# Router sums on two halves of the array's columns, and squares added by VectorE instead of GpSimd casts and TensorE sums

## The chip, the cores and the metric

One core of a Trainium2 chip runs the whole program: two transformer blocks on 512 tokens of width 1024, all in float32. The metric is the device time of one execution in microseconds (us). A difference is read against the median of the runs of the kernel before.

## The reference, cut to what matters

```python
# first block
mix = concat([attn, conv]) @ w_out
x = x + gt1 * mix                                   # x1, 8 row blocks of 128 columns, kept transposed
h2 = rms_norm(x, g_norm2) * (1 + sc2) + sh2
x = x + gt2 * hier_moe(h2, ...)                     # router: h2 @ [w_rg | w_re], 4 + 32 logits a token
x = rms_norm(x, g_final)
# second block
proj = rms_norm(h, norm_mix_pre) @ w_in             # among it the value projection sb_v
...
mix = (gate_sb * (sb @ w_sb_out) + gate_gla * (o @ w_gla_out)) @ w_o
h = h + rms_norm(mix, norm_mix_post)                # the mean of squares of mix, over 8 row blocks
ffn = (gelu(dwconv(rms_norm(h) @ w_up)) * (rms_norm(h) @ w_gate)) @ w_down
```

An RMS norm needs the sum of squares over all 1024 columns of a token. Activations lie transposed (columns on the 128 partitions), so such a sum runs across partitions and is made by TensorE: a product of a matrix of ones with the squares.

## The kernel before, in words

Weights stream from HBM through raw buffers. A class `Stream` splits each weight tile into a rounded part and a remainder (`split`, L223 on ScalarE and L224 by whichever engine `ws.lo` names), and a product in split form is three matmuls (`mm3`, L310 to L312). The order of instructions on each engine is set by a scheduler when the program is built; nobody writes it out. Within an engine, instructions run in that order.

Three places matter here.

**The router (L790 to L923).** For each of 8 row blocks m, the output projection of block m + 1 runs on TensorE (`pw` or `p`, L310 to L312) while VectorE and ScalarE turn block m into `x` (L793), `xs` (scaled, L796) and `sq` (squared, L798 or L800). Then `router` adds two float32 products: the logits, 36 columns of stationary weights, into bank `plg` (L808), and the sum of squares, 32 columns of ones, into another bank, `plq`, from partition 64 (L809). Four transposes `pth` (L817) follow. After the last block, ScalarE and VectorE copy the two sums into `lgT` (L919, L920), and `plgt` (L923) turns them over for the routing.

**The experts' end (L1419 to L1529).** After the experts, a loop over overflow blocks is branched over. Then the last expert's rows are added into x: pairs of products `psx` (L1306, L1307), VectorE's `x` (L1299), ScalarE's `sq` and `uh` and VectorE's `ul` (L1480). Sums of squares `pss` (L1276) and the second block's value projection (`pva`, `pvb`) run between them on TensorE. There `ws.lo` is GpSimd's `tensor_tensor`: GpSimd makes the remainder of four weight tiles, `wsplit`. GpSimd also makes `ut` (L1479). At the end VectorE works out the norm's factor (L1287 to L1292), builds a diagonal `dg` (L1526), and TensorE spreads it with `pspread` (L1529), twice.

**The mix before the feed-forward part (L2170 to L2200).** For each of 8 row blocks m and two column halves a (260 and 256 tokens), 24 matmuls make `pmix`; ScalarE reads it out twice, as `mx` (L2181) and as the square (L2182). A class `Sums` collects squares, and `flush` (L1641) adds each by a float32 product with ones, `psum` (L1643), after the next half's products. ScalarE (L1648) turns the sum into the norm's factor. Meanwhile the weights of block m + 2 are split into one of two `wsplit` tiles.

```python
    def mix_out(m, a):
        ps = pso.pop((m, a))
        act(part(mx[m], a), ps, AF.Copy, scale=cc("norm_mix_post", m))
        act(part(sqo[m], a), ps, AF.Square)
        su.add(a, sqo[m])
```

Of the kernel before, what the change touches and what calls it, by code (L numbers as in the profile page):

```python
# [11 lines left out]
F32 = mybir.dt.float32  # L12
# [3 lines left out]
OP = mybir.AluOpType  # L16
# [4 lines left out]
P = 128  # L21
T = 512
D = 1024
KD = D // P
NM = 16
L = T + NM
# [5 lines left out]


COLS = [
    ("b_mod", 48), ("g_norm1", 8), ("conv_b", 4), ("conv_ln_g", 4), ("conv_ln_b", 4),
    ("conv_w", 4 * 31), ("g_norm2", 8), ("w_router", 8 * 36), ("c", 8),
    ("g_final", 8), ("norm_mix_pre", 8), ("b_gk", 4), ("gla_head_norm", 2),
    ("norm_mix_post", 8), ("norm_ffn_pre", 8), ("conv_w2", 22 * 3), ("conv_b2", 22),
]
# [154 lines left out]
def build(nc, tc, I, out, dbg=None):  # L194
    with ExitStack() as ctx:
        _build(ctx, nc, tc, I, out, dbg or {})


def _build(ctx, nc, tc, I, out, dbg):
    mm = nc.tensor.matmul  # L200
    transpose = nc.tensor.transpose
    act = nc.scalar.activation
    tt = nc.vector.tensor_tensor
# [105 lines left out]
    def mm3(ps, lh, ll, rh, rl, first, last):  # L309
        mm(ps, lh, rh, start=first, stop=False)  # L310
        mm(ps, lh, rl, start=False, stop=False)  # L311
        mm(ps, ll, rh, start=False, stop=last)  # L312
# [10 lines left out]
    def cc(name, i=0, n=1):  # L323
        o = COFF[name][0] + i
        return cpk1[:, o:o + n] if o < NCOL1 else cpk2[:, o - NCOL1:o - NCOL1 + n]
# [5 lines left out]
    ones = const.tile([P, P], F32, name="ones")  # L331
# [44 lines left out]
    def p1(name="p1"):  # L376
        return pp.tile([P, 512], F32, name=name, tag="p1", bufs=4)
# [105 lines left out]
    ws = Stream(plan, castp, 3, nmoe)  # L483
# [62 lines left out]
    for k in range(KD):  # L546
        sq = big.tile([P, T], F32, name="sq", tag=("sq", "t512")[k % 2], bufs=2)
# [211 lines left out]
    wr = lambda k: cc("w_router", 36 * k, 36)  # L759
# [24 lines left out]
    plg = []  # L784
# [18 lines left out]
    def router(st):  # L803
        m, sq, xs = st
        if m == 0:
            plg.extend((p1("plg"), p1("plq")))
            act(rs_[:, 0, 0:1], sq[:, 0:1], AF.Sqrt)
        mm(plg[0][0:36, :], wr(m), xs, start=(m == 0), stop=(m == KD - 1), skip_group_check=True)  # L808
        mm(plg[1][64:96, :], ones[:, 0:32], sq, start=(m == 0), stop=(m == KD - 1), skip_group_check=True)  # L809
        if m < KD - 1:  # L810
            token_major(m, xs)

    def token_major(m, xs):
        pt = p1("pth")
        for i in range(4):
            s = slice(i * P, (i + 1) * P)
            transpose(pt[:, s], xs[:, s], ident)  # L817
        for a in range(2):
            (copy if m % 2 and m < KD - 1 else lambda o, x: act(o, x, AF.Copy))(
                h2t[a][:, :2 * D].rearrange("p (i d) -> p i d", d=D)[:, :, m * P:(m + 1) * P],  # L820
                pt[:, a * 256:(a + 1) * 256].rearrange("p (i n) -> p i n", n=P))
# [77 lines left out]
    for m in range(KD):  # L899
        if m < 6:  # L900
            ps = pw[m]
            proj1(ws, mh, ml, ps, k=4, k0=4, first=False)
        else:
            ps = p1()
            proj1(ws, mh, ml, ps)
        if m in (2, 5):
            with tc.high_priority(offset=-1000), tc.issue_after(tap[0].ins):
                for _ in range(2):
                    next(mod)
        if behind:  # L910
            router(behind)
        behind = ev_x1(m, ps)
    next(mod)
    router(behind)
    for m in range(KD):
        dump(f"x1_{m}", xT[m])
# [4 lines left out]
    plg = p1("plgt")[:, :256].rearrange("p (i n) -> p i n", n=64)  # L921
# [320 lines left out]
    def weighted(psd, w, spare=False):  # L1242
        yh, yl = [(ep.tile([P, D], F32R, name="yx", tag="x", bufs=3) if spare else
                   yp.tile([P, D], F32R, name=n, tag=n)) for n in ("yh", "yl")]
        for n in range(2):
            s = slice(n * 512, (n + 1) * 512)
            act(yh[:, s], psd[n], AF.Copy, scale=w)  # L1247
            stt(yl[:, s], psd[n], w, yh[:, s].bitcast(F32), OP.mult, OP.subtract)  # L1248
        return yh, yl
# [64 lines left out]
    side, xs = [], {}  # L1314
# [99 lines left out]
    last = weighted(psd, wsl[:, q:q + 1])  # L1414
# [4 lines left out]
    with tc.For_i(0, n_over, 1) as o:  # L1419
# [5 lines left out]
        ws = Stream([(I["w_moe"][bass.ds(e, 1), i, :, :].rearrange("a p n -> (a p) n"), (2048,), False)  # L1425
                     for i in range(6)])
# [13 lines left out]
    ws = main  # L1440
# [14 lines left out]
                self.t = raw1.tile([P, 2048], dt, name="wsplit", tag="raw", bufs=2)  # L1455
            return self.t[:, :1024] if tag == "whi" else self.t[:, 1024:]

    ws.pool, ws.rc, ws.rings, ws.lo = Halves(), 2, ws.rings[:1], nc.gpsimd.tensor_tensor
    ws.rings[0][3], ws.pin = len(plan), nmoe + 1
    ws.hold_at(nmoe + 2)  # L1460
    ws.load()
# [103 lines left out]
    HP = ctx.enter_context(tc.tile_pool(name="H", bufs=1))  # L1565
# [7 lines left out]
    def t5(name, p=P):  # L1573
        return HP.tile([p, L], F32, name=name, tag="t5", bufs=4)
# [52 lines left out]
    def part(ap, a):  # L1627
        return ap[:, E[a][0]:E[a][1]]

    class Sums:  # L1630
# [7 lines left out]
        def add(self, a, sq):  # L1638
            self.pend[a].append(sq)

        def flush(self, a):  # L1641
            for sq in self.pend[a]:
                mm(self.ps[a], ones, part(sq, a), start=(self.n[a] == 0), stop=(self.n[a] == KD - 1))  # L1643
                self.n[a] += 1
            self.pend[a] = []

# [72 lines left out]
    for k0 in (0, 4):  # L1719
        for x in (nh, nl):  # L1720
            for a in range(2):
                for k in range(4):
                    mm(pl[a][32 * k:32 * k + 32], w[:, k0 + k, :], x[k0 + k][:, a * HF:(a + 1) * HF].bitcast(F32),
                       start=(k0 == 0 and x is nh), stop=(k0 > 0 and x is nl), skip_group_check=True)
# [290 lines left out]
    last = gv0_end(gv[:, 0])  # L2015
# [3 lines left out]
    last = gv1_end(gv[:, 1])  # L2019
# [90 lines left out]
    for d in range(2):  # L2110
        sqs = []
# [5 lines left out]
        for a in range(2):  # L2117
            for h in range(4):
                mm(pn[32 * h:32 * h + 32, a, :H5], ones[:, 0:32], ends(sqs[h])[:, a], start=(d == 0), stop=(d == 1),
                   skip_group_check=True)  # L2120
# [45 lines left out]
    su = Sums([t[:, 0], t[:, 1]])  # L2166
    r = HP.tile([P, L], F32, name="rstd2", tag="rstd2", bufs=2)
    wo, pso, sqo = {}, {}, {}

    def mix_mm(m, a):  # L2170
        if m not in wo:
            wo[m] = ws.nxt(P)
            sqo[m] = t5("sq")
        wh, wl = wo[m]
        ps = pso[m, a] = p1("pmix")[:, :E[a][1] - E[a][0]]
        for kk in range(KD):
            mm3(ps, wh[:, kk, :], wl[:, kk, :], part(mh[kk], a), part(ml[kk], a), kk == 0, kk == KD - 1)

    def mix_out(m, a):
        ps = pso.pop((m, a))  # L2180
        act(part(mx[m], a), ps, AF.Copy, scale=cc("norm_mix_post", m))  # L2181
        act(part(sqo[m], a), ps, AF.Square)  # L2182
        su.add(a, sqo[m])

    for m in range(KD - 2):
        for a in range(2):
            mix_mm(m, a)
            su.flush(a)
        for a in range(2):
            mix_out(m, a)  # L2190

    for a in range(2):
        for m in (KD - 2, KD - 1):
            mix_mm(m, a)
            su.flush(a)
            mix_out(m, a)
        su.flush(a)
        with tc.high_priority(offset=100):
            su.rstd(a, r, D)
# [8 lines left out]
    def h_gen(a):  # L2208
        for k in range(KD):
            with tc.high_priority(offset=200):  # L2210
                t, h, g = cp.tile([P, T], F32, name="t", tag="y", bufs=3)[:, :E[a][1] - E[a][0]], part(hT[k], a), cc("norm_ffn_pre", k)
                tt(t, part(mx[k], a), part(r, a), OP.mult)
                (nc.gpsimd.tensor_tensor if k in HPL else tt)(h, h, t, OP.add)
                act(part(nh[k], a), h, AF.Copy, scale=g)
                stt(part(nl[k], a), h, g, part(nh[k], a).bitcast(F32), OP.mult, OP.subtract)
            sq = t5("sq")
            act(part(sq, a), h, AF.Square)
            su.flush(a)
            su.add(a, sq)
            if k == KD - 1:  # L2220
                su.flush(a)
            yield
# [20 lines left out]
    def ffn_mm(m):  # L2243
        ps, pg = p2("pup"), p1("pg")
        if m == 0:
            wg, ws.order = None, True
            for a in range(2):
                g = h_gen(a)
                for _ in range(1):
                    next(g)  # L2250
                if a == 0:
                    wu = ws.nxt(P)
                for n, _ in enumerate(up_gen(wu, ps, (a,))):
                    if n == 4 and wg is None:
                        wg = ws.nxt(P)
                    next(g, None)
                wg = wg or ws.nxt(P)
                run(gate_gen(wg, pg, slice(256 * a, 256 * a + 256)))
            ws.order = False
        else:  # L2260
            run(up_gen(ws.nxt(P), ps))
            run(gate_gen(ws.nxt(P), pg))
        return ps, pg
# [89 lines left out]
    su = Sums([p1("psum"), p1("psum")])  # L2353
# [29 lines left out]
```

## Time and profile before

| what | value |
|---|---|
| median of 3 runs | 1812.47 us (1812.36 to 1816.58) |
| profiled execution, its own time | 1818.69 us |
| span of the profiled execution | 1816.9 us, 26870 instructions |
| TensorE busy in the span | 1745.1 us (96%) |
| VectorE, ScalarE, GpSimd busy | 881.3, 629.3, 109.6 us |
| mean granted TensorE clock | 0.978 |

The span runs from the first instruction's start to the last one's end; the execution's own time has 1.8 us more around it. TensorE's busy time overstates it, since the ends of its pipelined matmuls are modelled: where matmuls follow each other, the distance of their starts is what one costs. A row of the timeline gives start, duration, engine, line, operation, output and inputs, the shape, how many instructions it merges, and in brackets how long the engine had been idle and what ended that.

### The profile page before, as it was taken

How to read it: one execution, taken by the hardware profiler on the slowest of the kernel's cores; microseconds unless marked ns; L12 is line 12 of the kernel's file. 1: busy time of each engine (PE TensorE's matmuls, PEld its weight loads, DVE VectorE, ACT ScalarE, POOL GpSimd, SP SyncE). 2: the span in 40 equal slices, each digit the busy share in tenths (PEclk: the TensorE clock that was granted, in tenths of full speed). 3: DMA queues.
4: the chain of work that ended last, by engine and by line, in shares of the span. 5: the costliest groups of instructions: out<-in, count | busy, mean ns of one | idle time of the engine just before them, and what ended most of it. 6: DMA issues, size and time to landing. Idle time of an engine off the chain costs nothing.

```text
span 1816.9 us, 26870 instructions
## 1 busy us (share of the span) xinstructions
PE 1745.1 (96%) x10826; PEld 1263.2 (70%) x10826; DVE 881.3 (49%) x1597; ACT 629.3 (35%) x1141; POOL 109.6 (6%) x147
## 2 busy tenths in 40 slices
PE   7999997999999999998899999999999999999997
PEld 4776565444445444445788668989999899789985
DVE  6789654433333334235577742253332645335534
ACT  5226653211111111104567743242233633223322
POOL 2000010000000000003200100030000111001101
PEclk9989898999999999999999999999999999999998
DMA  8563253999999999930411012113222222222221
GB/s 327 199 242 136 89 216 130 380 409 409 408 411 360 385 408 410 412 128 27 159 67 49 24 47 93 47 63 128 102 100 87 70 91 78 100 93 93 94 87 64
DMA packets 73986, 328.01 MB, mean 181 GB/s; under 512 B 8019, under 2 KB 8403, under 8 KB 59652
## 3 DMA queue, kind: packets, MB, share of 16 engines
q1 hardware_dynamic: 72608, 320.36, 46.6%
q0 software_dynamic: 1248, 5.91, 0.9%
q8 instruction: 86, 1.41, 0.3%
q14 instruction: 40, 0.33, 0.0%
q10 hardware_dynamic: 4, 0.00, 0.0%
HBM read 321.98 MB, written 4.26 MB: 180 GB/s over the span
## 4 chain that ended last, share of the span: by engine, by line
PE 48%; DVE 3%; ACT 2%; DMA 1%; POOL 1%; issue 1%; DVEq 0%; ACTq 0%; POOLq 0%
PE p L1620 11%; PE pup L2232 7%; PE pq L1598 4%; PE pg L312 2%; PE pg L310 2%; PE pg L311 2%; PE pd L311 2%; PE pd L312 2%; PE pd L310 2%; PE pv L310 1%; PE pv L311 1%; PE pv L312 1%; PE pmix L310 1%; PE psum L1643 1%; PE pmix L312 1%; PE pmix L311 1%
## 5 line engine op out<-in xcount | busy, mean ns | idle before, releaser
L224 DVE TENSOR_TENSOR wsplit<-raw,wsplit 128x1024 fp32r<-128x1024 f32 (+1 forms) x140 | 167.4, 1198 | 250.6 <-ACT wsplit L223 244.7
L223 ACT ACTIVATE wsplit<-raw 128x1024 fp32r<-128x1024 f32 (+1 forms) x144 | 146.8, 1022 | 260.5 <-PE pd L312 76.3
L1206 PE MATMUL pgu<-raw,x 128*64 128x512 f32 x960 | 220.3, 598 | 0.0
L1206 PEld LDWEIGHTS pgu<-raw,x 128*64 128x64 f32 x960 | 64.1, 136 | 119.9 <-issue 106.4
L1299 DVE SCALAR_TENSOR_TENSOR x<-psx,modc,x 128x512 f32<-128x512 f32 x136 | 93.2, 745 | 50.1 <-PE psx L1307 50.0
L1248 DVE SCALAR_TENSOR_TENSOR yl<-pdn,wsl,yh 128x512 fp32r<-128x512 f32 x34 | 25.4, 751 | 178.8 <-ACT yh L1247 178.3
L1206 PE MATMUL pdn<-raw,hT 128*64 128x512 f32 x480 | 105.7, 593 | 0.7 <-ACT hT L1228 0.7
L1228 ACT ACTIVATE hT<-pht 128x512 f32<-128x512 f32 x17 | 10.2, 597 | 232.0 <-PE pht L1222 227.5
L1206 PEld LDWEIGHTS pdn<-raw,hT 128*64 128x64 f32 x480 | 34.5, 137 | 69.1 <-issue 64.4
L647 DVE SCALAR_TENSOR_TENSOR y<-u,cpk,y 128x512 f32<-128x512 f32 x116 | 80.6, 748 | 0.1
L311 PE MATMUL pd<-wsplit,ah 128*128 128x512 f32 x176 | 71.1, 404 | 2.1 <-DVE wsplit L224 2.0
L1168 PE MATMUL psg<-oh,h2h 128*128 128x256 f32 (+1 forms) x288 | 67.8, 292 | 3.1 <-DVE oh L1153 3.1
L1620 PE MATMUL p<-nha,wsplit 128*128 128x258 f32 x384 | 69.0, 293 | 1.3 <-ACT wsplit L223 0.7
L312 PE MATMUL pd<-wsplit,al 128*128 128x512 f32 x176 | 70.1, 398 | 0.0
L310 PE MATMUL pd<-wsplit,ah 128*128 128x512 f32 x176 | 68.9, 397 | 0.9 <-ACT wsplit L223 0.9
L1168 PE MATMUL psg<-oh,h2l 128*128 128x256 f32 (+1 forms) x288 | 65.7, 282 | 0.0
L1620 PE MATMUL p<-nhb,wsplit 128*128 128x258 f32 x384 | 65.6, 283 | 0.0
L2232 PE MATMUL pup<-nha,wsplit 128*128 128x258 f32 x352 | 64.0, 291 | 0.4 <-ACT wsplit L223 0.4
L1306 PE MATMUL psx<-ohT,yh 128*128 128x512 f32 x136 | 59.3, 436 | 5.2 <-ACT wsplit L223 5.1
L2232 PE MATMUL pup<-nhb,wsplit 128*128 128x258 f32 x352 | 63.2, 287 | 0.0
L1168 PEld LDWEIGHTS psg<-oh,h2h 128*128 128x128 f32 x288 | 53.6, 196 | 9.7 <-issue 5.7
L1620 PEld LDWEIGHTS p<-nha,wsplit 128*128 128x128 f32 x384 | 56.2, 195 | 3.0 <-ACT wsplit L223 0.9
(653 smaller groups left out, 3973.5 us busy)
## 6 DMA issues: line engine op xcount, KB each, us to landing
raw<-w_moe SPq DMA_DIRECT2D x312, 512.0 KB, 10.1
raw<-w_moe SPq DMA_DIRECT2D x36, 1024.0 KB, 10.0
raw<-w_ff SPq DMA_DIRECT2D x22, 1024.0 KB, 4.8
raw<-w_mod SPq DMA_DIRECT2D x16, 1024.0 KB, 5.9
raw<-w_qk SPq DMA_DIRECT2D x12, 1024.0 KB, 5.1
raw<-w_v SPq DMA_DIRECT2D x8, 1024.0 KB, 4.9
raw<-w_modk SPq DMA_DIRECT2D x8, 1024.0 KB, 5.2
raw<-w_mg SPq DMA_DIRECT2D x8, 1024.0 KB, 4.9
```

Of the source, the lines that this page charges most:

```text
L223: act(hi, src, AF.Copy)
L224: return sub(lo, src, hi.bitcast(F32), OP.subtract)
L310: mm(ps, lh, rh, start=first, stop=False)
L311: mm(ps, lh, rl, start=False, stop=False)
L312: mm(ps, ll, rh, start=False, stop=last)
L647: tap[0] = stt(y[:, m, :], src, w, y[:, m, :], OP.mult, OP.add)
L1168: fix(mm(ps[k // 2][:, k % 2 * 256:][:, :n], w[i][:, k * P:(k + 1) * P], oh[:, i, :n], start=(i == 0 and w is h2h and k % 2 == 0), stop=(i ...
L1206: fix(mm(ps[s, :], l[:, s], w[:, 2 * b + i, :], start=first, stop=last, skip_group_check=True))
L1299: stt(xT[m], ps, gt2(m), xT[m], OP.mult, OP.add)
L1598: mm(ps[a], l[:, kk, :], r[kk][:, a * HF:(a + 1) * HF], start=(kk == 0 and fl == 0), stop=(kk == k - 1 and fl == 2))
L1620: mm(ps[a], l[:, kk, :], ends(r[kk])[:, a], start=(kk == 0 and fl == 0), stop=(kk == k - 1 and fl == 2))
L2232: mm(ps[:, a, :HC], l[:, kk, :], x[kk][:, o:o + HC], start=(kk == 0 and fl == 0), stop=(kk == KD - 1 and fl == 2))
```

## The change

The router's two products both get 64 columns of stationary weights, for partitions 0 to 63 and 64 to 127. The 28 columns behind a block's 36 are whatever lies there; rows 36 to 63 of `plg` are not read. So that the last block's 64 columns exist in the packed constants, `w_router` moves ahead in the list. At the experts' end `ws.lo` becomes VectorE's `tensor_tensor`. In the mix, the square of block 0 gets a tile of its own (`sqs`), VectorE adds the squares of blocks 1 to 5 into it, and TensorE sums `sqs` once where it summed six tiles; blocks 6 and 7 are summed as before. `flush` gets its last product marked by its caller.

```diff
 COLS = [
-    ("b_mod", 48), ("g_norm1", 8), ("conv_b", 4), ("conv_ln_g", 4), ("conv_ln_b", 4),
-    ("conv_w", 4 * 31), ("g_norm2", 8), ("w_router", 8 * 36), ("c", 8),
+    ("b_mod", 48), ("g_norm1", 8), ("w_router", 8 * 36), ("conv_b", 4), ("conv_ln_g", 4), ("conv_ln_b", 4),
+    ("conv_w", 4 * 31), ("g_norm2", 8), ("c", 8),
...
-        mm(plg[0][0:36, :], wr(m), xs, start=(m == 0), stop=(m == KD - 1), skip_group_check=True)
-        mm(plg[1][64:96, :], ones[:, 0:32], sq, start=(m == 0), stop=(m == KD - 1), skip_group_check=True)
+
+        mm(plg[0][0:64, :], cc("w_router", 36 * m, 64), xs, start=(m == 0), stop=(m == KD - 1), skip_group_check=True)
+        mm(plg[1][64:128, :], ones[:, 0:64], sq, start=(m == 0), stop=(m == KD - 1), skip_group_check=True)
...
-    ws.pool, ws.rc, ws.rings, ws.lo = Halves(), 2, ws.rings[:1], nc.gpsimd.tensor_tensor
+    ws.pool, ws.rc, ws.rings, ws.lo = Halves(), 2, ws.rings[:1], tt
...
-        def flush(self, a):
+        def flush(self, a, last=True):
             for sq in self.pend[a]:
-                mm(self.ps[a], ones, part(sq, a), start=(self.n[a] == 0), stop=(self.n[a] == KD - 1))
+                mm(self.ps[a], ones, part(sq, a), start=(self.n[a] == 0), stop=last)
...
-            sqo[m] = t5("sq")
+            sqo[m] = t5("sq") if m else HP.tile([P, L], F32, name="sqs", tag="rstd2", bufs=2)
...
         act(part(sqo[m], a), ps, AF.Square)
-        su.add(a, sqo[m])
+        if 0 < m < KD - 2:
+            tt(part(sqo[0], a), part(sqo[0], a), part(sqo[m], a), OP.add)
+        if m == 0 or m == KD - 2:
+            su.pend[a] = [sqo[0]] if m == 0 else su.pend[a] + [sqo[m]]
+        elif m == KD - 1:
+            su.add(a, sqo[m])
 
     for m in range(KD - 2):
         for a in range(2):
             mix_mm(m, a)
-            su.flush(a)
         for a in range(2):
             mix_out(m, a)
 
     for a in range(2):
         for m in (KD - 2, KD - 1):
             mix_mm(m, a)
-            su.flush(a)
+            su.flush(a, False)
             mix_out(m, a)
```

On TensorE at the router's end, before the change (block 6's pair and transposes, then block 7's pair, then the turn-over):

```order
L808 MATMUL plg<-xs_2112,cpk_67 36x512
L809 MATMUL plq<-sq_2111,ones 32x512
L817 MATMUL pth<-ident,xs_2112 128x128 x4
L809 MATMUL plq<-sq_2150,ones 32x512
L808 MATMUL plg<-xs_2151,cpk_67 36x512
L923 MATMUL plgt<-selr,lgT 128x37 x4
```

The same place in the changed kernel:

```order
L809 MATMUL plg<-xs_2112,cpk_67 64x512
L810 MATMUL plq<-sq_2111,ones 64x512
L818 MATMUL pth<-ident,xs_2112 128x128 x4
L810 MATMUL plq<-sq_2150,ones 64x512
L809 MATMUL plg<-xs_2151,cpk_67 64x512
L924 MATMUL plgt<-selr,lgT 128x37 x4
```

The order is the same; each of the eight pairs has 64 columns twice instead of 36 and 32.

On VectorE at the experts' end, before the change, from the branch over the loop on:

```order
L1299 SCALAR_TENSOR_TENSOR x_70<-psx,modc,x_70 128x512 x4
L1299 SCALAR_TENSOR_TENSOR x_71<-psx,modc,x_71 128x512
L1480 SCALAR_TENSOR_TENSOR ul<-x_70,gfp,uh 128x512 x4
L1299 SCALAR_TENSOR_TENSOR x_71<-psx,modc,x_71 128x512
L1480 SCALAR_TENSOR_TENSOR ul<-x_71,gfp,uh 128x512 x2
```

In the changed kernel, from the same branch on:

```order
L1300 SCALAR_TENSOR_TENSOR x_70<-psx,modc,x_70 128x512 x2
L224 TENSOR_TENSOR wsplit<-raw,wsplit 128x1024 x2
L1481 SCALAR_TENSOR_TENSOR ul<-x_70,gfp,uh 128x512
L1300 SCALAR_TENSOR_TENSOR x_70<-psx,modc,x_70 128x512
L1481 SCALAR_TENSOR_TENSOR ul<-x_70,gfp,uh 128x512
L1300 SCALAR_TENSOR_TENSOR x_70<-psx,modc,x_70 128x512
```

Two remainder casts now stand behind the second `x` and ahead of the third. The other two come later: one ahead of the last `ul`, one ahead of the second reciprocal of the norm's factor. On TensorE the fifth `psx` pair moves behind two `pss` pairs and eight products of the value projection, and the first `pspread` behind `psr` and three more products.

On VectorE in the mix, before the change (the six casts of blocks 2 to 7, then the work behind the norm's factor):

```order
L224 TENSOR_TENSOR wsplit<-raw,wsplit 128x1024 x6
L2212 TENSOR_TENSOR t<-mxa,rstd_11228 128x260 x2
L2213 TENSOR_TENSOR hTa<-hTa,t 128x260 x2
```

In the changed kernel (the casts of blocks 2, 3 and 4 with the first additions):

```order
L224 TENSOR_TENSOR wsplit<-raw,wsplit 128x1024
L2185 TENSOR_TENSOR sqs<-sqs,sq 128x260
L2185 TENSOR_TENSOR sqs<-sqs,sq 128x256
L224 TENSOR_TENSOR wsplit<-raw,wsplit 128x1024
L2185 TENSOR_TENSOR sqs<-sqs,sq 128x260
L2185 TENSOR_TENSOR sqs<-sqs,sq 128x256
L224 TENSOR_TENSOR wsplit<-raw,wsplit 128x1024
```

Ten additions stand between the casts, two ahead of each of the last five. On TensorE ten `psum` products are gone, one behind each half of blocks 1 to 5; from block 6 on, the sums stand where they stood.

## Rows read from the trace of the kernel before

**Rows 1.** Windows by stage; columns as in the first line.

```profile
core 0: us, PE busy (x) PEld busy (x) DVE busy (x) ACT busy (x) POOL busy (x), PEclk, DMA share, GB/s
252.00:296.00 44.00, 43.32 (x167) 23.46 (x166) 12.55 (x19) 15.11 (x28) 0.00 (x0) 1.00 0.19 67
...
316.00:806.00 490.00, 490.00 (x2350) 229.22 (x2350) 181.01 (x390) 70.58 (x135) 0.00 (x0) 1.00 0.97 382
...
821.30:849.00 27.70, 27.49 (x121) 15.57 (x121) 17.04 (x21) 13.75 (x22) 13.89 (x12) 0.94 0.08 32
...
1361.00:1411.00 50.00, 50.00 (x396) 48.80 (x395) 12.23 (x19) 20.41 (x44) 1.16 (x2) 1.00 0.25 86
```

**Rows 2.** Timeline of TensorE: the router's first pair and what follows it.

```profile
252.15 1.05 PE L808 MATMUL plg<-xs,cpk 128*36 128x512 f32 x2
...
254.10 0.66 PE L817 MATMUL pth<-ident,xs 128*128 128x128 f32 x4
```

**Rows 3.** Timeline of all engines at the router's end.

```profile
290.31 0.72 ACT L796 ACTIVATE xs<-x,a 128x512 f32<-128x512 f32 x1 [6.90 <-DVE x L793]
...
291.90 1.05 PE L809 MATMUL plq<-sq,ones 128*32 128x512 f32 x2
...
292.88 1.05 PE L808 MATMUL plg<-xs,cpk 128*36 128x512 f32 x2
292.98 0.69 DVE L920 COPY lgT<-plq 32x512 f32<-32x512 f32 x1 [1.97 <-PE plq L809]
...
294.60 1.08 PE L923 MATMUL plgt<-selr,lgT 128*128 128x37 f32 x8 [0.68 <-ACT lgT L919]
```

**Rows 4.** Timeline of TensorE: one expert's down projection, 16 products of two passes each.

```profile
809.14 7.14 PE L1206 MATMUL pdn<-raw,hT 128*64 128x512 f32 x32 [0.75 <-ACT hT L1228]
```

**Rows 5.** Timeline of TensorE: 32-column products in one bank, then in two.

```profile
826.05 0.62 PE L1276 MATMUL pss<-sq,ones 128*32 128x512 f32 x1
826.06 0.62 PE L1276 MATMUL pss<-sq,g2r 128*32 128x512 f32 x1
...
827.03 0.50 PE L310 MATMUL pva<-wsplit,uh 128*128 128x512 f32 x1
...
865.32 0.41 PE L1723 MATMUL pl<-nhb,raw 128*32 128x264 f32 x1 [1.22 <-ACT nhb L1662]
865.33 0.43 PE L1723 MATMUL pl<-nha,raw 128*32 128x264 f32 x3
```

**Rows 6.** Timeline of all engines at the end of the experts' end.

```profile
846.99 2.38 POOL L224 TENSOR_TENSOR wsplit<-raw,wsplit 128x1024 fp32r<-128x1024 f32 x1 [6.05 <-ACT wsplit L223]
...
847.35 2.05 DVE L1292 TENSOR_TENSOR rs__80<-rs__80 128x4 f32<-128x4 f32 x1
...
850.27 1.10 PE L1529 MATMUL pspread<-dg,ones 128*128 128x512 f32 x2 [1.22 <-DVE dg L1526]
...
854.46 1.02 PE L1529 MATMUL pspread<-dg,ones 128*128 128x512 f32 x2
...
855.59 2.06 DVE L1661 SCALAR_TENSOR_TENSOR nt<-x,gfp,pspread 128x512 f32<-128x512 f32 x3 [3.67 <-PE pspread L1529]
...
871.75 0.48 PE L1598 MATMUL pq<-nha,wsplit 128*128 128x264 f32 x2 [1.09 <-DVE x L1666]
```

**Rows 7.** The page's part 5: the remainder cast on VectorE (busy us, mean ns).

```profile
L224 DVE TENSOR_TENSOR wsplit<-raw,wsplit 128x1024 fp32r<-128x1024 f32 (+1 forms) x140 | 167.4, 1198 | 250.6 <-ACT wsplit L223 244.7
```

**Rows 8.** Timeline of TensorE and VectorE in the mix.

```profile
1364.38 0.29 PE L310 MATMUL pmix<-mha,wsplit 128*128 128x260 f32 x1
...
1367.26 0.60 PE L1643 MATMUL psum<-sq,ones 128*128 128x260 f32 x2
...
1372.47 1.23 DVE L224 TENSOR_TENSOR wsplit<-raw,wsplit 128x1024 fp32r<-128x1024 f32 x1 [4.93 <-ACT wsplit L223]
...
1400.05 0.60 PE L1643 MATMUL psum<-sq,ones 128*128 128x260 f32 x2
```

**Rows 9.** Instructions of line 2212: min, median, max ns.

```profile
L2212 DVE TENSOR_TENSOR t<-mxa,rstd x8: 418/420/430, 1406.1 to 1418.1; 128x260 f32<-128x260 f32 x4, 128x256 f32<-128x256 f32 x4
```

More of the change, by code (lines that the diff above doesn't have):

```diff
@@ L2217, in h_gen @@
             act(part(sq, a), h, AF.Square)
-            su.flush(a)
+            su.flush(a, False)
             su.add(a, sq)
```

## The prediction, made before the changed kernel ran

> **What bounds the kernel now.** I read the windows by stage first, because the three edits lie in three stages and a gain counts only where the shortened engine sets the pace. [rows 1] TensorE is busy in 43.32 of the 44 us around the router, in 27.49 of 27.7 us after the experts' branch and in all 50 us of the mix; the other engines work well under half of these stretches, except VectorE at the experts' end (17.04 of 27.7). So TensorE sets all three. The expert stage between, 490 us, has TensorE and the DMA engines (0.97) both full, so nothing inside it can absorb or add time if it merely starts earlier. Its weights wait for buffers that the router's end and the first expert products free, so its dates follow from where the router ends. Then I read the timelines at the three places.
>
> **Router.** The first pair starts at 252.15 and the transposes behind it at 254.10 [rows 2]: 1.95 us for two float32 products. In the last pair the second starts 0.98 us behind the first (291.90, 292.88) [rows 3]: with 36 and 32 columns the two run one after the other. Do 64-column halves run together? The nearest row is the experts' down projection, 32 passes of 128 rows by 64 columns on 512 tokens, in 7.14 us [rows 4]. Sixteen products by 0.98 one after the other would be 15.7 us; two together are 8 × 0.89. Two 32-column products into one bank also start 0.01 us apart, and the next product follows 0.98 us after the first (826.05, 827.03) [rows 5]. That our two outputs lie in different banks is no obstacle either: a product on `nhb` and three on `nha`, which write the two banks of `pl`, start 0.01 us apart at 865.32 [rows 5]. So a pair falls from 1.95 to 0.98, the pair with its switches in and out: 0.97 us saved.
>
> Seven pairs stand between products of the output projection: 7 × 0.97 = 6.8 us. They are TensorE time as long as `xs` and `sq` are ready. Between a block's last product and its router pair stand three elementwise steps like the 0.72 us scaling [rows 3], 2.2 us (estimate); TensorE spends at least the next block's 12 products of about 0.24 us (24 products of 260 tokens take 1367.26 − 1364.38 = 2.88 us [rows 8], scaled to 512), 2.9 us. Cover 0.7 us and more; without it a pair would lose what is missing. The eighth pair is on the path: its second product would start at 291.90, both sums would end near 292.9, and VectorE's copy, 292.98 to 293.67 [rows 3], would be the later of the two. `plgt` would follow at 293.7 instead of 294.60: 0.9 us. Sum 7.7. Bounds: 0 if the halves wait for each other; 8 × (1.95 − 0.89) = 8.5 if a pair runs at the rate of [rows 4].
>
> The Trainium skill speaks against this in "TensorE: Matmul & The Clock Gate", Part 3, The mechanism: a weight load overlaps products in flight only where the row group differs, and ours share all 128 rows. By that rule the pair stays at 1.95 us and this term is 0; this case's down projection, at 0.89 a pair [rows 4], does not agree with it.
>
> **Experts' end.** GpSimd's fourth cast runs from 846.99 to 849.37, and a VectorE operation on 4 elements a partition, started at 847.35, ends at 849.40: 2.05 us, with GpSimd's end. The diagonal behind it is late and TensorE idles 1.22 us before `pspread` [rows 6]. Without GpSimd there that operation is short. Its cast, 1.2 us on VectorE [rows 7], now stands ahead of the second reciprocal, and ends near 848.1 if it starts where GpSimd's did; two small steps and the diagonal (some 1 us, estimate from the gap 849.40 to 850.27) end near 849.2. TensorE meanwhile has `psr` and three products, about 1.0 us, that moved ahead of `pspread`, and needs the diagonal only near 850.1. So the 1.22 us go. Of the 0.2 us that TensorE idles in 821.3 to 849 [rows 1], and of small waits hidden in the spacing, I take 0.3 more, since the remainder of the first tile is ready before TensorE reaches it. Sum 1.5.
>
> The price stands on VectorE: two casts, 2.4 us [rows 7], ahead of the third `x`. Behind it wait the third `ul`, the square of the third block, and the fifth `psx` pair, which needs the third's bank. But two `pss` pairs (0.98 each) and eight products (0.24 each), 3.9 us, now stand on TensorE ahead of that fifth pair, so it hides; if not, up to 2.4 us are lost. Bounds: 1.5 + 0.3 gained, 2.4 lost.
>
> What is gained reaches the next stage: the second `pspread` starts at 854.46, VectorE's next chain at 855.59 waited for it, and TensorE at 871.75 waited for VectorE [rows 6]. All three move together. GpSimd keeps its small `ut` operations, which stand beside VectorE's casts. The Trainium skill ("GPSIMD Engine Reference", 8. Key points) says that GpSimd and a VectorE operation with two inputs in SBUF contend; the 2.05 us agree in kind, and I add nothing for it.
>
> **Mix.** From the first sum at 1367.26 to the eleventh at 1400.05 [rows 8] stand ten half-blocks of 24 products with one sum each: 3.28 us a piece. One without a sum, 1364.38 to 1367.26, took 2.88 (260 tokens; 256 give 2.84, scaled). Ten sums at 3.28 − 2.86: 4.2 us off TensorE. Added: ten VectorE additions of 0.42 us [rows 9], while VectorE is busy 12.23 of 50 us [rows 1]. Each waits for ScalarE's square, and behind the second stands the cast of a block two ahead. That cast waits for ScalarE's rounded half anyway, which ScalarE makes after the same square; the row cast begins at 1372.47 and ends at 1373.70 [rows 8], about 3.2 us after its half-block's end, and its products begin two half-blocks after that end, 5.7 us without sums. Cover 2.5 us. The last block's sums and ScalarE's factor behind them stand as before. The tile `sqs` takes a buffer whose last reader is long done. Bounds: 4.4 and, if casts come late, a loss (below).
>
> **Sum.** 7.7 + 1.5 + 4.2 = 13.4 us. On the profiled execution's own 1818.69 that is 1805.3. The median is 6.2 us below that execution, whatever the reason, and I take the same difference off it: 1812.47 − 13.4 = **1799.1 us**.
>
> **The rivals.**
> - *Halves wait for each other.* For it: no product of 64 columns with both its streams and its banks apart stands in this trace. Against: [rows 4, 5]. The router gives nothing: 1812.47 − 5.7 = 1806.8 us. The Trainium skill's rule on row groups, cited above, would have this case.
> - *VectorE is late at the experts' end.* For it: its program order. The 1.5 us are not gained and 2.4 lost: 1799.1 + 3.9 = 1803.0.
> - *The experts' weights keep their dates.* If the stream were held by something other than the router's end, 7.7 us would be eaten in the 490 us that DMA fills [rows 1]: 1806.8. Against: the buffers that TensorE frees start it.
> - *Slower: late casts in the mix.* If an addition holds the cast of a block until after its products should start, TensorE waits once a block, in five blocks. It outweighs the whole gain of 13.4 us where each wait passes 2.7 us, so where each cast comes 2.5 + 2.7 = 5.2 us later than now; at 3 us a wait the time is 1799.1 + 15 = 1814.1. To pass 0.3% it takes 3.8 us a wait: 1818. Nothing in the rows makes an addition that late.
>
> **How the numbers follow.** All three gains 0.68, halves wait 0.11, VectorE late 0.12, weights keep their dates 0.05, slower 0.04. Likeliest: 1799.1, on its own 1796 to 1801.5 (the upper bounds 8.5, 1.8 and 4.4 together give 1797.8, and I leave a little for the median, whose three runs spread over 4 us). The range goes from 1795.5 up to 1807.0, so that only the slower case and mixtures are left out. A measurement tells 0.3%, 5.4 us, from no change: the line is 1807.0. The two cases at 1806.8 lie on it, and I give half of each to either side: faster 0.88, same 0.09 with a little of the slower case, slower 0.03.
>
> **What would show it.** Right: `plq` starts within 0.05 us of `plg`, transposes 0.98 us behind; `plgt` 7.7 us earlier; the 4-element operation back under 0.3 us and no wait of TensorE at the first `pspread`; half-blocks of the mix at 2.86 us without idle. Wrong: pairs of starts 0.98 apart; TensorE waiting for `x` at a `psx` or for `sq` at a `pss`; waits for `wsplit` in the mix; or an expert stage longer than 490 us.

## The result and the profile after

The changed kernel took 1800.95 us, median of 6 runs, against 1812.41 us for 6 runs of the kernel before; the ratio is 0.9922 [0.9902, 0.9942], so 14 us faster with some 4 us to either side. One of the 6 runs, of 2835.52 us at a mean granted clock of 0.557, was disturbed and is not in the ratio; the median of the other five is 1800.32 us. The profiled execution took 1800.32 us (span 1798.5, 26848 instructions, mean granted clock 0.980).

The windows of the changed kernel, laid over the same four stretches as [rows 1], the first and the last cut to the stages' new lengths:

```profile
core 0: us, PE busy (x) PEld busy (x) DVE busy (x) ACT busy (x) POOL busy (x), PEclk, DMA share, GB/s
246.40:281.60 35.20, 34.34 (x155) 21.49 (x154) 12.47 (x19) 14.86 (x27) 0.00 (x0) 1.00 0.23 83
310.00:800.00 490.00, 489.25 (x2348) 229.63 (x2345) 179.21 (x365) 68.71 (x131) 0.00 (x0) 1.00 0.96 379
809.20:836.90 27.70, 27.65 (x126) 16.39 (x127) 17.27 (x26) 14.08 (x22) 8.58 (x8) 0.93 0.08 29
1344.00:1392.20 48.20, 48.20 (x394) 47.49 (x394) 18.83 (x32) 21.28 (x46) 1.38 (x3) 1.00 0.29 99
```

TensorE still fills nearly all of them; the work left out is gone from the engine that sets the pace. GpSimd's share at the experts' end fell from 13.89 to 8.58 us, VectorE's in the mix rose to 18.83, still under half.

Between marks that are in both traces (the first router pair, `plgt`, the first `psx` behind the branch, the first `pq`, the first `pmix`, the first `pup`, the end), the stages were this long, in us:

| kernel | ahead of router | router | experts | experts' end | attention | mix | rest |
|---|---|---|---|---|---|---|---|
| before | 252.15 | 42.45 | 526.74 | 50.41 | 486.85 | 52.45 | 405.85 |
| after | 246.45 | 35.18 | 527.62 | 48.59 | 486.14 | 48.26 | 406.26 |

The three changed stages lost 7.27 + 1.82 + 4.19 = 13.28 us. The profiles differ by more, 18.4 us, because 5.70 us went ahead of the router, in unchanged code. The windows of that stretch, before and after:

```profile
200.00:240.00 40.00, 38.31 (x178) 24.28 (x177) 24.33 (x55) 20.90 (x46) 0.00 (x0) 0.91 0.60 233
```

```profile
200.00:240.00 40.00, 37.72 (x187) 26.18 (x187) 27.41 (x58) 23.56 (x45) 0.00 (x0) 1.00 0.66 257
```

The granted clock, the third number from the end of the row, was 0.91 there in the profile before and 1.00 in the one after. That this is no part of the change is seen over the twelve profiles of this case: the five with 0.83 to 0.91 in this stretch (before and four experiments) reach the router at 251.3 to 254.2 us, the seven with 1.00 (after and six experiments) at 245.8 to 248.1, with and without each part of the change. Why the clock was lower in some executions, no run here shows.

**Router.** The changed kernel's timeline of TensorE at the first pair [rows 2], then of all engines at the end [rows 3]:

```profile
246.45 0.64 PE L809 MATMUL plg<-xs,cpk 128*64 128x512 f32 x1
246.45 0.64 PE L810 MATMUL plq<-sq,ones 128*64 128x512 f32 x1
246.93 0.59 PE L809 MATMUL plg<-xs,cpk 128*64 128x512 f32 x1
246.93 0.59 PE L810 MATMUL plq<-sq,ones 128*64 128x512 f32 x1
247.46 0.66 PE L818 MATMUL pth<-ident,xs 128*128 128x128 f32 x4
...
279.69 0.64 PE L810 MATMUL plq<-sq,ones 128*64 128x512 f32 x1
279.71 0.64 PE L809 MATMUL plg<-xs,cpk 128*64 128x512 f32 x1
...
280.80 0.69 DVE L921 COPY lgT<-plq 32x512 f32<-32x512 f32 x1 [1.16 <-PE plg L809]
...
281.63 1.05 PE L924 MATMUL plgt<-selr,lgT 128*128 128x37 f32 x8 [0.85 <-DVE lgT L921]
```

A float32 product is two passes here, each a line of its own above. Both halves' first passes start together, the second passes 0.48 us later, the transposes 1.01 us behind the pair instead of 1.95. The weights of both passes of `plq` load while the first pass of `plg` runs (timeline of TensorE's weight loads):

```profile
246.45 0.13 PEld L810 LDWEIGHTS plq<-sq,ones 128*64 128x64 f32 x1
...
246.51 0.14 PEld L810 LDWEIGHTS plq<-sq,ones 128*64 128x64 f32 x1
```

**Experts' end.** Timeline of VectorE and TensorE of the changed kernel, the place of [rows 6]:

```profile
834.41 1.23 DVE L224 TENSOR_TENSOR wsplit<-raw,wsplit 128x1024 fp32r<-128x1024 f32 x1 [1.65 <-ACT wsplit L223]
835.55 0.17 DVE L1292 RECIPROCAL rs__80<-rs__80 128x4 f32<-128x4 f32 x1
835.76 0.17 DVE L1293 TENSOR_TENSOR rs__80<-rs__80 128x4 f32<-128x4 f32 x1
835.96 0.69 DVE L1527 TENSOR_TENSOR dg<-ident,rs__80 128x512 f32<-128x512 f32 x1
836.41 0.50 PE L1555 MATMUL psr<-rs__80,shift 128*128 128x5 f32 x4
...
837.57 1.02 PE L1530 MATMUL pspread<-dg,ones 128*128 128x512 f32 x2
840.53 1.02 PE L1530 MATMUL pspread<-dg,ones 128*128 128x512 f32 x2
841.66 2.06 DVE L1662 SCALAR_TENSOR_TENSOR nt<-x,gfp,pspread 128x512 f32<-128x512 f32 x3 [3.95 <-PE pspread L1530]
```

The operation on 4 elements takes 0.17 us instead of 2.05, and `pspread` has no wait in brackets, where it had 1.22.

**Mix.** Timeline of TensorE of the changed kernel, its first product and its first sum:

```profile
1343.98 0.36 PE L310 MATMUL pmix<-mha,wsplit 128*128 128x260 f32 x1 [0.88 <-DVE g L2152]
...
1381.21 0.60 PE L1644 MATMUL psum<-sqs,ones 128*128 128x260 f32 x2
```

Thirteen half-blocks without a sum stand between them: 37.23 us, 2.864 each, no idle (the whole mix window is 48.20 busy of 48.20). With a sum each a half-block took 3.28 [rows 8].

### The profile page after: what moved, and what is told of

It reads as the page before. It is cut to its first block, busy times and chain, and to the rows that moved or that the text cites. A ratio compares the mean times of both kernels' runs of the same rounds, so it can differ in the third digit from the quotient of the medians.

```text
span 1798.5 us, 26848 instructions
## 1 busy us (share of the span) xinstructions
PE 1726.3 (96%) x10806; PEld 1255.1 (70%) x10806; DVE 884.0 (49%) x1611; ACT 629.2 (35%) x1141; POOL 102.7 (6%) x143
## 4 chain that ended last, share of the span: by engine, by line
PE 49%; DVE 3%; ACT 2%; POOL 1%; issue 0%; DVEq 0%; ACTq 0%; POOLq 0%
PE p L1621 11%; PE pup L2237 7%; PE pq L1599 5%; PE pg L312 2%; PE pg L310 2%; PE pg L311 2%; PE pd L311 2%; PE pd L312 2%; PE pd L310 2%; PE pv L310 1%; PE pv L312 1%; PE pv L311 1%; PE pmix L310 1%; PE pmix L312 1%; PE pmix L311 1%; PE psb L1892 1%
## 5 line engine op out<-in xcount | busy, mean ns | idle before, releaser
L224 DVE TENSOR_TENSOR wsplit<-raw,wsplit 128x1024 fp32r<-128x1024 f32 (+1 forms) x144 | 171.9, 1196 | 228.8 <-ACT wsplit L223 222.8
```

The source lines that it names most:

```text
L224: return sub(lo, src, hi.bitcast(F32), OP.subtract)
```

## The experiments

The first three put one part of the change alone into the kernel before, to see whether its gain is made in its own stage and stays. Their times stand beside 25 runs of the kernel before on that chip, median 1815.16 us.

**e1_router: the router alone.** The constants reordered as in the change, and

```diff
-        mm(plg[0][0:36, :], wr(m), xs, ...
-        mm(plg[1][64:96, :], ones[:, 0:32], sq, ...
+        mm(plg[0][0:64, :], cc("w_router", 36 * m, 64), xs, ...
+        mm(plg[1][64:128, :], ones[:, 0:64], sq, ...
```

> The router's 64-column pairs alone, on the kernel before. Theory (halves of the same width run together, and nothing else in the whole change touches this place): from the first router product to the turn-over product 35.2 us as in the changed kernel, where before has 42.45; both other places as before (50.4 us from the experts' branch to the next stage's first product, 52.45 us of mix); the whole about 7.3 us shorter, 0.996. Rival (the router's gain is eaten by the expert stage, whose weights keep their dates): the router 35.2 us, but from the turn-over to the first product behind the experts' branch 534 instead of 526.7 us, and the whole time unchanged.

Measured: 1809.02 us, ratio 0.9965 [0.9939, 0.9991]; router 35.19 us, experts 527.43, experts' end 50.48 and mix 52.47 as before. The stream of weights does not eat the gain: the experts' stage would have to be 7 us longer and is 0.69 longer than before. That 0.69 is not the earlier start either, since e2 with the router of before has 527.36.

**e2_cast: the remainder casts alone.**

```diff
-    ws.pool, ws.rc, ws.rings, ws.lo = Halves(), 2, ws.rings[:1], nc.gpsimd.tensor_tensor
+    ws.pool, ws.rc, ws.rings, ws.lo = Halves(), 2, ws.rings[:1], tt
```

> The four remainder casts on VectorE alone, on the kernel before. Theory: from the experts' branch's first product to the first product of the next stage 48.6 us instead of 50.4, no wait of TensorE at the first spread product, router 42.45 and mix 52.45 us as before; the whole 1.8 us shorter, which is below what a timing can tell. Rival (the 1.8 us come from the router's earlier end or the mix, not from the casts): 50.4 us stay.

Measured: 1812.48 us, ratio 0.9983 [0.9962, 1.0005], not told from no change by the runs; but the experts' end is 48.56 us, with the router at 42.46 and the mix at 52.48 as before.

**e3_mix: the mix alone** (the changed kernel with router, constants and casts as before).

> The squares added by VectorE alone, on the kernel before. Theory: from the first product of the mix to the first product behind it 48.3 us instead of 52.45, half-blocks of 2.86 us without waits, the other two places as before; the whole 4.2 us shorter, 0.998. Rival (a part of the mix's gain is a lower price of the two clock levels or of the earlier stage): less than 4 us here.

Measured: 1812.84 us, ratio 0.9982 [0.9959, 1.0005], not told from no change by the runs; but the mix is 48.28 us, 4.17 less than before, so the rival's less than 4 us did not come. Its experts' end, unchanged code, took 51.31 instead of 50.41. The windows from the first `psx` of that stage on, in the kernel before and in e3:

```profile
821.34:827.34 6.00, 5.83 (x15) 2.72 (x15) 4.11 (x6) 4.04 (x8) 3.96 (x4) 0.72 0.28 117
```

```profile
816.00:822.00 6.00, 6.00 (x12) 2.85 (x14) 3.62 (x5) 3.96 (x8) 3.89 (x4) 0.50 0.24 100
822.00:825.00 3.00, 3.00 (x12) 0.99 (x9) 3.00 (x4) 1.81 (x4) 3.00 (x4) 0.92 0.00 0
```

TensorE had waited 5.06 us ahead of this stage in the kernel before and 5.36 in e3. Over the first 6 us e3 is granted 0.50, its level of 1.2 GHz, the kernel before 0.72 and the other ten profiles 0.63 to 0.72. That the clock lengthened the stage is argued from these rows; no edit of e3 lies ahead of it.

**Which widths run together?** In e4 only the sum of squares goes back to 32 columns; e5 and e10 are the other crossings.

```diff
-        mm(plg[1][64:128, :], ones[:, 0:64], sq, ...
+        mm(plg[1][64:96, :], ones[:, 0:32], sq, ...      # e4_sum32
...
-        mm(plg[0][0:64, :], cc("w_router", 36 * m, 64), xs, ...
+        mm(plg[0][0:36, :], wr(m), xs, ...               # e5_log36 and e10_sum33
...
-        mm(plg[1][64:128, :], ones[:, 0:64], sq, ...
+        mm(plg[1][64:97, :], ones[:, 0:33], sq, ...      # e10_sum33
```

> The changed kernel with the sum of squares back at 32 columns, partitions 64 to 95, and the logits at 64 columns. It separates two reasons for which 36 and 32 columns ran one after the other. If both products must have the same width to run together: pairs of 1.95 us and a router of about 42 us again. If only the odd width 36 stood in the way, and 32 columns can run beside 64: pairs of about 1.0 us and a router of 35.2 us.

> The changed kernel, but the logits keep their 36 columns of stationary weights (partitions 0 to 35) beside a sum of squares of 64 columns (partitions 64 to 127). Theory (two products run together only when both have the same number of columns): they run one after the other, a pair takes 1.95 to 1.98 us, and the router stage, from its first pair to its turn-over, takes about 42.5 us as in the kernel before. Rival (what matters is that the second product fills a whole half of the array): the second starts within 0.05 us of the first, a pair takes 1.0 us, the stage 35.2 us.

> The logits with 36 columns of stationary weights on partitions 0 to 35 as before the change, the sum of squares with 33 columns on partitions 64 to 96: one column more than before, nothing else different in the router. The earlier runs had 36 beside 32 and 64 beside 32 one after the other (pairs of 1.95 and 1.98 us) and 36 beside 64 together. Theory (a product of up to 32 columns is set up in another partition of the array than one of 33 to 64; two products run together when both are of the same kind, however many columns each has): the second product starts within 0.05 us of the first, a pair takes 1.0 us, the router 35.2 us. Rival (the second product must fill its half of the array, or 64 columns are needed in one of them): the pair takes 1.95 us, the router 42.5 us.

The first pair and the transposes behind it, in e4_sum32, e5_log36 and e10_sum33 (timelines of TensorE):

```profile
254.22 1.07 PE L809 MATMUL plg<-xs,cpk 128*64 128x512 f32 x2
255.22 1.04 PE L810 MATMUL plq<-sq,ones 128*32 128x512 f32 x2
256.20 0.66 PE L818 MATMUL pth<-ident,xs 128*128 128x128 f32 x4
```

```profile
251.89 0.62 PE L809 MATMUL plg<-xs,cpk 128*36 128x512 f32 x1
251.89 0.64 PE L810 MATMUL plq<-sq,ones 128*64 128x512 f32 x1
...
252.90 0.66 PE L818 MATMUL pth<-ident,xs 128*128 128x128 f32 x4
```

```profile
248.07 0.62 PE L809 MATMUL plg<-xs,cpk 128*36 128x512 f32 x1
248.07 0.62 PE L810 MATMUL plq<-sq,ones 128*33 128x512 f32 x1
...
249.05 0.66 PE L818 MATMUL pth<-ident,xs 128*128 128x128 f32 x4
```

64 beside 32 columns: one after the other, pair 1.98 us, router 42.67, one run of 1814.39 us. 36 beside 64: together, 1.01, router 35.19, 1805.91 (a run of before beside it: 1807.74). 36 beside 33: together, 0.98, router 35.00, 1797.59 (8 runs of before beside it: median 1815.65). After e4 I held that both must have the same number of columns; e5 ended that theory. With 32 beside 32 together [rows 5] and 36 beside 32 apart [rows 2], all six cases fit one statement: a product of up to 32 columns and one of 33 to 64 do not run side by side, two of one kind do. The Trainium skill ("TensorEngine Tiling (Array Packing)", Tiling Modes, Key Properties) says that a change of the tiling mode, not of the tile alone, drains TensorE; the six cases agree, if 32 columns are one mode and 33 to 64 the next. That reading is argued, the six pair times are measured.

**What gives the 1.8 us at the experts' end?** The change does four things there at once: two early casts leave GpSimd, two late ones do, and on TensorE the fifth `psx` pair moves, and `psr` and three products move ahead of the first `pspread`. e6 gives the first two casts back to GpSimd, e7 the last two (there `pspread` also stands where it stood before), e8 all four but with `psr` and the three products moved. The fifth `psx` pair goes with the early casts in every trace: in e6 and e8 it stands where it stood before the change, so their TensorE has the order of the changed kernel only from the last `ps` products on, and not in the whole stage as their expectations say.

```diff
-    ws.pool, ws.rc, ws.rings, ws.lo = Halves(), 2, ws.rings[:1], tt
+    n_lo = [0]
+
+    def lo_by(*a):
+        n_lo[0] += 1
+        return (nc.gpsimd.tensor_tensor if n_lo[0] < 3 else tt)(*a)      # e7: the two swapped
+    ws.pool, ws.rc, ws.rings, ws.lo = Halves(), 2, ws.rings[:1], lo_by
...
-    rr = spread(rs_[:, 2, 1:5], pns)          # e8, with ws.lo = nc.gpsimd.tensor_tensor
     psr = psx("psr")
...
-    vsteps(4)
+    vsteps(1)
+    rr = spread(rs_[:, 2, 1:5], pns)
+    vsteps(3)
```

> The changed kernel, but the first two remainder casts of the experts' end go back to GpSimd; the last two stay on VectorE, and TensorE's order is that of the changed kernel. Theory (the gain comes from GpSimd's last cast no longer stretching VectorE's 4-element operation): from the first psx to the first pq of the attention 48.6 us (to 48.9), the 4-element operation 0.17 us. Rival (the early casts matter as much): 49.5 us or more.

> The mirror: the first two remainder casts on VectorE as in the changed kernel, the last two on GpSimd as before; TensorE's first spread product stands directly where it stood before the change. Theory: the 4-element operation takes about 2 us again, TensorE waits about 1.2 us for the diagonal, and the stretch from the first psx to the first pq takes about 50.4 us. Rival (the early casts matter): 48.6 to 49.5 us.

> The changed kernel, but all four remainder casts of the experts' end on GpSimd, with TensorE's order as in the changed kernel: psr and three products of the value projection ahead of the first spread product. It parts two reasons for the 1.8 us of that stage that the change brings together. Theory (the GpSimd cast beside VectorE's small operation costs the time, the order covers a part): the 4-element operation takes about 2 us, the stretch 49.3 to 49.7 us. Rival A (the order alone gives it all): 48.6 us though the operation is long. Rival B (the order gives nothing): 50.4 us.

I cut the stage at ScalarE's `rs` behind the last `ps` product (L1286 before, L1287 after). The marks in the timelines of TensorE and ScalarE, before (its `pq` stands in [rows 6]) and after:

```profile
821.34 0.72 PE L1306 MATMUL psx<-ohT,yh 128*128 128x512 f32 x1 [5.06 <-ACT wsplit L223]
...
844.30 0.27 ACT L1286 ACTIVATE rs__80<-ps,epsb 128x4 f32<-128x4 f32 x1 [0.45 <-PE ps L1284]
```

```profile
809.25 0.79 PE L1307 MATMUL psx<-ohT,yh 128*128 128x512 f32 x1 [5.30 <-ACT wsplit L223]
...
831.82 0.27 ACT L1287 ACTIVATE rs__80<-ps,epsb 128x4 f32<-128x4 f32 x1 [0.45 <-PE ps L1285]
...
857.84 0.78 PE L1599 MATMUL pq<-nha,wsplit 128*128 128x264 f32 x2 [1.08 <-DVE x L1667]
```

| kernel | first psx to rs | rs to first pq | sum | early casts with fifth psx pair, late casts, order of psr and pspread |
|---|---|---|---|---|
| before | 22.96 | 27.45 | 50.41 | GpSimd, GpSimd, before |
| e8_order | 23.05 | 26.65 | 49.70 | GpSimd, GpSimd, moved |
| e7_first_two | 22.63 | 27.39 | 50.02 | VectorE, GpSimd, before |
| e6_last_two | 23.04 | 26.02 | 49.06 | GpSimd, VectorE, moved |
| after | 22.57 | 26.02 | 48.59 | VectorE, VectorE, moved |

In the first part early casts on VectorE, with the order of `psx` that comes with them, give about 0.4 us, whatever the late ones do: over all profiles the first part is 22.53 to 22.65 us with them and 22.96 to 23.05 without (e3, with its lower clock, 23.87). Whether the casts or the moved pair give it was not taken apart. In the second part the moved order alone gives 0.80 us (27.45 to 26.65) and the late casts 0.63 more (to 26.02). So the theory on record for these runs fell short: e8 came out as it said, but e6 lies 0.16 us above its bound and e7 0.4 below its number, both by the first part, which it had left out; the rivals' numbers were not reached either. And the wait behind GpSimd is worth less than its 1.22 us once other products stand in it. e8's timeline shows that:

```profile
840.27 2.38 POOL L224 TENSOR_TENSOR wsplit<-raw,wsplit 128x1024 fp32r<-128x1024 f32 x1 [6.05 <-ACT wsplit L223]
...
840.63 2.05 DVE L1293 TENSOR_TENSOR rs__80<-rs__80 128x4 f32<-128x4 f32 x1
...
842.73 0.61 PE L1553 MATMUL psr<-rs__80,shift 128*128 128x5 f32 x4 [0.40 <-DVE rs__80 L1293]
...
843.98 1.02 PE L1530 MATMUL pspread<-dg,ones 128*128 128x512 f32 x2
```

The long operation is back, 2.05 us to GpSimd's end, but TensorE waits 0.40 us for it instead of 1.22. The fourth corner, late casts on VectorE with the order of before, was not run, so how much the late casts alone would give is open. The single times were 1799.25 (e6), 1799.93 (e7) and 1806.90 us (e8), beside one run of before of 1807.74; e8 is one of the five with the lower clock ahead of the router.

**e9_seven: one more square on VectorE.** The changed kernel, with block 6's square added too, so that TensorE sums two tiles a half instead of three.

```diff
-        if 0 < m < KD - 2:
+        if 0 < m < KD - 1:
...
-        if m == 0 or m == KD - 2:
-            su.pend[a] = [sqo[0]] if m == 0 else su.pend[a] + [sqo[m]]
+        if m == KD - 2:
+            su.pend[a] = [sqo[0]]
```

> The changed kernel, with VectorE adding the square of block 6 as well, so that TensorE sums two tiles a half (sqs and block 7) where it sums three. Theory (TensorE sets the pace of the mix): two sums of 0.42 us less, the mix from its first product to the feed-forward part's first product 47.4 us instead of 48.26, and the stages behind it as long as before, a gain of 0.8 us that only the stage lengths can show. Rival (the norm's factor behind the last sums sets the end): the mix is shorter but TensorE then waits longer for the factor or the normed rows, and mix and rest together stay at 454.5 us.

Measured: 1797.28 us, ratio to before 0.9924 [0.9890, 0.9957], where the change itself has 0.9922. The mix took 48.02 us where the theory had 47.4, the rest 406.82: together 454.84, against 454.52 in the changed kernel and 454.2 to 455.5 over the eight profiles whose mix is that of the change. So the gain of 0.8 us did not come, as the rival said. Its reason is not shown, because the order at the seam between the mix and the feed-forward part moved too. Timelines of TensorE at the seam, in the changed kernel and in e9, then of VectorE in e9:

```profile
1392.24 0.39 PE L2237 MATMUL pup<-nha,wsplit 128*128 128x258 f32 x1
...
1395.25 0.92 PE L1644 MATMUL psum<-sq,ones 128*128 128x256 f32 x3 [2.07 <-ACT sq L2183]
```

```profile
1388.68 0.39 PE L2237 MATMUL pup<-nha,wsplit 128*128 128x258 f32 x1 [0.24 <-ACT wsplit L223]
...
1392.00 1.23 PE L1644 MATMUL psum<-sq,ones 128*128 128x260 f32 x2 [2.81 <-ACT sq L2222]
1393.03 1.06 PE L1644 MATMUL psum<-sqs,ones 128*128 128x256 f32 x2
```

```profile
1392.21 0.41 DVE L2185 TENSOR_TENSOR sqs<-sqs,sq 128x256 f32<-128x256 f32 x1
```

In the changed kernel TensorE waits 2.07 us for ScalarE's square of the mix's last block (L2183). In e9 it waits 2.81 us, and for a square of the feed-forward part (L2222); the sum `sqs` of the second half stands behind that wait, at 1393.03, and VectorE adds block 6's square to it only at 1392.21. In this order nothing was won from the last sums; what another order would give was not run.

## Why the prediction was right

The median came 1.9 us above the forecast 1799.1, inside the range, and below the time of every rival. The three stages gave 13.28 us where the sum had 13.4; that they lie so close is luck in part, since the router gave 0.43 less and the experts' end 0.32 more. The terms:

- **Router, 7.7 forecast, 7.27 measured.** The halves run together, as read from [rows 4]. From the first pair to the last, 6.51 us went, where 7 × 0.97 = 6.8 was taken: a pair is 1.01 us, not 0.98. At the end `plgt` follows the last pair's start by 1.94 us instead of 2.70 [rows 3], 0.76 and not 0.9: I let it start 0.03 us behind VectorE's copy, and it starts 0.14 behind (280.80 + 0.69, then 281.63). The cover of 0.7 us for `xs` and `sq` held: of the 0.86 us in which TensorE is not busy in the router's window, 0.85 stand ahead of `plgt`.
- **The reason given for the halves** was right in part only. I asked whether halves of 64 columns run together, and took the widening of both products for the cause; what mattered was 32 columns against 33 or more in the second (e5, e10). Widening the logits, for which the constants moved, did nothing for the time: one more column in the sum of squares does the whole of it (e10, with the constants still moved). The Trainium skill ("TensorE: Matmul & The Clock Gate", Part 3, The mechanism) says that weights load beside running products only where row groups differ. This case does not agree: both halves share all 128 rows, the weights of `plq` load at 246.45 and 246.51 while the first pass of `plg` runs (246.45, 0.64 us), and the halves' passes start 0.00 to 0.02 us apart.
- **Experts' end, 1.5 forecast, 1.82 measured.** The first part of the stage gave 0.39, where I had taken 0.3 for the early casts; I had left out that the moved `psx` pair could be a part of it. The second part gave 1.43, where I had taken the 1.22 of the wait. That wait went for two reasons, and I had named one: the three products and `psr`, which I counted only as cover, are worth 0.80 us while GpSimd still holds VectorE (e8), the end of that hold 0.63 more. The price, two casts ahead of the third `x`, was hidden as worked out: TensorE is busy 27.65 of 27.70 us there. One reading of [rows 1] was loose: ScalarE and GpSimd were busy 13.75 and 13.89 of 27.7 us there, which is half and not well under it; no term used it.
- **Mix, 4.2 forecast, 4.19 measured.** Ten sums of 0.42. No product of `pmix` waits for `wsplit`, so the casts' cover of 2.5 us stood; the additions took 0.43 us each.
- **What was gained stayed.** The experts' stage is 0.88 us longer than before, but 0.62 longer in e2 too, where nothing ahead of it changed; the attention stage is 0.71 shorter, and lay between 481.70 and 486.85 over the twelve profiles. Neither can be charged to the change. The 490 us that I named as a sign were the length of a window inside that stage and could not tell this; the stage between its marks does.

The medians differ by 11.5 us, and the ratio gives 14.1. I put the distance of both from 13.28 down to the stages that the change does not touch: between the two profiles the largest such difference is the 5.7 us ahead of the router.

## What to carry to other kernels

When two narrow float32 products stand side by side, look at their start times in the trace, and try one column more or fewer before any larger rearrangement: here 33 columns beside 36 cost half of 32 beside 36. Read a gain by the length of its stage between marks that both traces have, because here the unchanged code ahead of the first mark moved by nearly as much as the two smaller parts together. And where a change removes a wait, look whether it also moved something into that wait, and try the two apart. Compare each engine's order in the trace of an experiment with that of the kernel it is to explain: e6, e8 and e9 moved more on TensorE than their edits name.

## What the runs showed of the hardware

- Two products over all 128 rows, on different columns of the array and into different banks, can run at the price of one, 0.98 us [rows 3]: 0.98 to 1.01 us a pair for 36 and 33, 36 and 64, 64 and 64 columns, against 1.95 to 1.98 for 36 and 32, 64 and 32.
- The hold between VectorE and GpSimd goes both ways. GpSimd's cast stretched a VectorE operation on 4 elements from 0.17 to 2.05 us; with the casts on VectorE, one of GpSimd's small `ut` operations, 0.36 to 0.81 us each in the kernel before, took 2.31 us. The timelines of GpSimd and VectorE in the changed kernel:

```profile
811.37 0.36 POOL L1480 TENSOR_SCALAR ut<-x,gfp 128x32 f32<-128x32 f32 x1 [3.49 <-DVE x L1300]
812.21 2.31 POOL L1480 TENSOR_SCALAR ut<-x,gfp 128x32 f32<-128x32 f32 x1 [0.48 <-DVE x L1300]
```

```profile
812.03 2.35 DVE L224 TENSOR_TENSOR wsplit<-raw,wsplit 128x1024 fp32r<-128x1024 f32 x2
```

The second `ut` started 0.18 us behind VectorE's two casts and ended with them, at 814.5 against 814.4. Nobody waited for it. The Trainium skill ("GPSIMD Engine Reference", 8. Key points) names this contention for VectorE operations with two inputs in SBUF; both casts are of that kind, and the trace agrees.
